# A decoder layer on one core: the first normalisation reads a transposed copy of x instead of transposing it on TensorE

## The chip, the cores and the metric

The kernel runs on one core of one Trainium2 chip. A core has TensorE (PE in the profile, with its weight loads as PEld), VectorE (DVE), ScalarE (ACT), GpSimd (POOL) and SyncE (SP, which here only issues transfers), and 16 DMA engines that they all share. The metric is the device time of one execution in microseconds (us); lower is better. The time of a kernel is the median of its runs.

## The reference

One decoder layer over 256 tokens of 2048 channels, in float32. Only its first steps matter here:

```python
h = rmsnorm(x, norm_mix_pre[l])
proj = h @ w_in[l]
xr, yr, q, k, v, g_rnn, g_attn = jnp.split(proj, IN_OFFSETS, axis=-1)
...
q = rope(q.reshape(B, S, N_Q_HEADS, HEAD_DIM), positions)
k = rope(k.reshape(B, S, N_KV_HEADS, HEAD_DIM), positions)
...
def rmsnorm(x, g):
    xf = x.astype(jnp.float32)
    y = xf * lax.rsqrt(jnp.mean(xf * xf, axis=-1, keepdims=True) + RMS_EPS)
    return (y * g.astype(jnp.float32)).astype(x.dtype)
```

After that come a gated linear recurrence over xr and yr, sliding-window attention over q, k and v, the merge of both by the gates, an output projection and an MLP with 8192 hidden channels, each with its own normalisation.

## The kernel before

**Products in parts.** Every large product is made from float32 operands that are split in a high part (rounded to the type that TensorE multiplies in one pass) and a low part (the rest), and sums three of the four products of parts. For the weights the class `Stream` does this: it cuts each weight chunk of 128 partitions x 2048 numbers (1 MiB) into two halves of 512 KiB, loads them in a fixed order on SP's queue (`load_to`, L76), and splits each into `whi` (a copy on ACT, L94 or L103) and `wlo` (a subtraction on DVE, L95 or L111). Halves 0 to 9 have rooms of their own; from half 10 on there is a ring of four (`WRAW`). The split halves have rings of six (`WHALF`). `ahead(j)` splits up to half j + 5 and asks for loads up to ten halves past j, as the rings allow.

**The activations.** TensorE contracts over the partitions, so x has to stand with its channels on the partitions, as 16 tiles of 128 channels x 256 tokens: `hT`, again in a high and a low part, already multiplied by the gain g of the normalisation (`gcol`). The factor 1/rms of each token is not in hT; it is put in behind the products.

**The beginning, before.** x comes in as it lies, tokens on the partitions (`x_nat`, two blocks tb of 128 tokens, in four quarters of 512 channels each), interleaved on SP's queue with the first weight halves. `turn(tb, q)` transposes one quarter of a block on TensorE (four transposes of 128x128, L375) into PSUM. `part(tb, q)` makes the parts of hT from PSUM: high on ACT (L382), low on DVE (L385), one instruction for each tile of 128 channels and block of 128 tokens, 32 on each engine. `kv_step(j)` takes the weight half j and two channel tiles, and makes 12 products of 128x128 by 128x512 (L396): eight with `whi` and then four with `wlo`. Eight such steps make keys and values. The transposes for the steps 2q + 2 and 2q + 3 stand between the steps 2q and 2q + 1. Most of this is held in program order by `keep_in_program_order` (`pin`): such an instruction stays behind the one written before it on its engine. What is not pinned is ordered when the program is built, by when it is expected to be ready.

**The squares.** The sums of squares of x for 1/rms are taken from x_nat ahead of the last kv step: block 0 in four instructions on ACT (L405), block 1 in four on DVE (L403).

**The pass behind it.** `b_pass512` runs 8 weight halves of 12 products each (L294, L296, L298), first for a group of gates (`g`), then for a group of queries (`q`). After each half of a gate pass it calls `pump`, which runs the next piece of the generators that wait: the first is `keys_values`, which calls `first_norm` (sum and root of the squares with `rms`, L357 to L359; 1/rms into the rotary tables cc and ss, L445; the spread of 1/rms over all partitions by a product with ones, L448, and its copy to `rT`), and for each token block copies the values (L519), rotates the keys (`rope`, L505 to L509) and transposes them on TensorE (`pk`, L526) into `kT`. The small inputs (positions, frequencies, sinks, per-channel vectors) are loaded on SP's queue behind the first 14 weight halves.

Of the kernel before, what the change touches and what calls it, by code (L numbers as in the profile page):

```python
# [30 lines left out]
NH, NKV, HD = 32, 4, 64  # L31
# [132 lines left out]
EXTRA = 5  # L164


def layer(tc, x, g_pre, pos_t, pos_row, inv_freq, vecs, sinks, gains, w_kv, w_q, w_xy, w_rg, w_g, w_rp, w_ap, w_out,
          w_up, w_dn, out):
    nc = tc.nc
    ctx = ExitStack()  # L170
# [7 lines left out]
    mm = nc.tensor.matmul  # L178
# [43 lines left out]
    def bank(pool, name):  # L222
        return pool.tile([P, 512], F32, tag=pool.name, name=name)
# [100 lines left out]
    def t2(name, dt=F32):  # L324
        return pa.tile([P, 512], dt, tag="t2", bufs=T2, name=name)

    x_nat = [flat(unit(f"x{tb}", F32)) for tb in range(TB)]
# [4 lines left out]
    gcol = const.tile([P, KT], F32, name="gcol")  # L332
    nc.scalar.dma_start(gcol, g_pre)

    for q in range(4):
        nc.sync.dma_start(x_nat[0][:, quarter(q)], x_v[0][:, quarter(q)])
        if q == 0:
            ws.load_to(1)
        last = nc.sync.dma_start(x_nat[1][:, quarter(q)], x_v[1][:, quarter(q)])
        with tc.issue_after(last.ins):  # L340
            ws.load_to(2 * q + 2)
# [8 lines left out]
    nc.vector.memset(ones, 1.0)  # L350
# [15 lines left out]
        mm(warm[:, 0:P], ones, ones, start=True, stop=True)  # L366
    hT = units("hT")
    pin = ws.pin = tc.keep_in_program_order
    ps_t = {}

    def turn(tb, q):
        ps = ps_t[tb, q] = bank(psm, "ptr")
        for i in range(4):
            k = 4 * q + i
            pin(nc.tensor.transpose(ps[:, i * P : i * P + P], x_nat[tb][:, k * P : k * P + P], ident))  # L375

    def part(tb, q, ks=range(4)):
        t = slice(tb * P, tb * P + P)
        ps = ps_t[tb, q]
        for i in ks:  # L380
            g = gcol[:, 4 * q + i : 4 * q + i + 1]
            pin(nc.scalar.activation(hT[q][:, i, 0, t], ps[:, i * P : i * P + P], AF.Copy, scale=g))  # L382
        for i in ks:
            g = gcol[:, 4 * q + i : 4 * q + i + 1]
            pin(nc.vector.scalar_tensor_tensor(hT[q][:, i, 1, t], ps[:, i * P : i * P + P], g,  # L385
                                               hT[q][:, i, 0, t].bitcast(F32), ALU.mult, ALU.subtract))

    kv = [bank(psb, f"kv{tb}") for tb in range(TB)]

# [8 lines left out]

    def squares(tb):
        for q in range(4):  # L400
            x, into = x_nat[tb][:, quarter(q)], sq[:, 0, tb, q : q + 1]
            if tb:
                pin(nc.vector.scalar_tensor_tensor(t2("j"), x, 1.0, x, ALU.mult, ALU.mult, accum_out=into))  # L403
            else:
                pin(nc.scalar.activation(t2("j"), x, AF.Square, accum_out=into))  # L405

    turn(0, 0)
    turn(1, 0)
    part(0, 0, (0, 1))
    ws.split_high()  # L410
    part(1, 0, (0, 1))
    ws.split_low()
    for tb in range(TB):
        part(tb, 0, (2, 3))
    ws.split_to(2)
    for q in range(4):
        kv_step(2 * q)
        if q < 3:
            turn(0, q + 1)
            turn(1, q + 1)  # L420
            part(0, q + 1)
            part(1, q + 1)
            ws.split_to(2 * q + 4)
        else:
            ws.pin = lambda i: i
            squares(0)
            squares(1)
            ws.split_to(2 * q + 4)
        kv_step(2 * q + 1)
    ws.ahead(ws.at - 1)  # L430
    r0, r0h = [], []
    rT = pa.tile([P, S], F32, name="rT")

    def first_norm():

        pr = bank(psm, "pr")
        spread = t2("spread")
        for tb in range(TB):
            r = rms(tb, 0)
            half = st[:, 16 + tb : 17 + tb]  # L440
            nc.vector.tensor_scalar(half, r, 0.5, None, ALU.mult)
            r0.append(r)
            r0h.append(half)
            for t in (cc, ss):
                nc.vector.tensor_scalar(t[:, tb], t[:, tb], r, None, ALU.mult)  # L445
            dg = spread[:, tb * P : tb * P + P]
            nc.vector.tensor_scalar(dg, ident, r, None, ALU.mult)
            mm(pr[:, tb * P : tb * P + P], ones, dg, start=True, stop=True)  # L448
        nc.scalar.copy(rT, pr[:, 0:S])

    pos_i = pa.tile([P, TB], I32, name="pos_i")
    nc.sync.dma_start(pos_i, pos_t)
    ifr = pa.tile([P, 32], F32, name="ifr")
    nc.sync.dma_start(ifr, inv_freq.partition_broadcast(P))
    sink = pa.tile([P, NH], F32, name="sink")
    nc.sync.dma_start(sink, sinks.partition_broadcast(P))
    vec = pa.tile([P, 8, KT], F32, name="vec")
    nc.sync.dma_start(vec, vecs.rearrange("p (a b) -> p a b", a=8))


    mask1 = pa.tile([P, S], F32, name="mask1")
    nc.gpsimd.memset(mask1, 0.0)
# [51 lines left out]

    def keys_values(banks):
        yield
        first_norm()
        for tb in range(TB):
            nc.scalar.activation(v_sb[:, tb, :], banks[tb][:, 256:512], AF.Copy, scale=r0[tb])  # L519
            k2 = t2("k2")  # L520
            k4 = k2.rearrange("p (g c d) -> p g c d", g=NKV, c=2)
            rope(banks[tb][:, 0:256], tb, NKV, [k4[:, :, 0, :], k4[:, :, 1, :]])
            yield
            ps = bank(psm, "pk")
            for g in range(NKV):
                nc.tensor.transpose(ps[:, g * P : g * P + P], k2[:, g * P : g * P + P], ident)  # L526
# [711 lines left out]
def lay_out(inp):  # L1238


    def a_type(w):
        k, n = w.shape
        return np.ascontiguousarray(w.reshape(KT, P, n // P, P).transpose(2, 1, 0, 3)).reshape(n // P, P, 2048)

    def b_type(w, cols):
        k, n = w.shape
        per = 2048 // cols
        t = w.reshape(k // (per * P), per, P, n // cols, cols).transpose(3, 0, 2, 1, 4)
        return np.ascontiguousarray(t).reshape(-1, P, 2048)
# [23 lines left out]
    return {  # L1273
        "x": np.asarray(inp["x"]).reshape(S, D),
        "g_pre": per_channel(g("norm_mix_pre")),
        "pos_t": pos.T,
        "pos_row": pos.reshape(S),
        "inv_freq": (10000.0 ** (-np.arange(0, HD, 2, dtype=np.float64) / HD)).astype(np.float32),
        "vecs": np.concatenate(vecs, axis=1),
        "sinks": g("attn_sinks").reshape(NKV, 4, 2).transpose(0, 2, 1).reshape(NH),  # L1280
        "gains": np.stack([g(n) for n in ("norm_mix_pre", "norm_mix_post", "norm_mlp_pre", "norm_mlp_post")]),
        "w_kv": b_type(kv, 512),
        "w_q": b_type(q, 512),
        "w_xy": a_type(np.concatenate([xr, yr], axis=1)),
        "w_rg": np.ascontiguousarray(rg).reshape(4, P, 2048),
        "w_g": b_type(gg, 512),
        "w_rp": b_type(g("w_rnn_proj"), 512),
        "w_ap": b_type(g("w_attn_proj"), 512),
        "w_out": b_type(g("w_out"), 1024),
        "w_up": a_type(g("w_mlp_up")),  # L1290
        "w_dn": np.concatenate([down(w_dn[:4096]), down(w_dn[4096:])]),
    }
# [15 lines left out]
```

## Time and profile before

| what | value |
|---|---|
| runs | 1514.89, 1511.7, 1516.5 us; median 1514.89 us |
| span of the profiled execution | 1515.7 us |
| TensorE clock granted | 0.998 |
| PE busy | 1493.5 us (99%), 7600 instructions |
| DVE busy | 1102.2 us (73%) |
| ACT busy | 829.2 us (55%) |
| HBM read | 288.60 MB, 195 GB/s over the span |

The profile is that of one execution. A row of the timeline gives the start, the time from the first to the last instruction merged in the row, the engine, the line, the operation, out<-in, the shapes and the count, and in brackets the idle time just ahead of it with what ended it. A matmul's row shows its whole way through the array, so its time is longer than the distance to the next one; the pace of TensorE is read from the starts. Groups of instructions show the busy time and the mean of one in ns, and behind it the idle time of the engine ahead of them.

### The profile page before, as it was taken

To read this page: it belongs to the slowest core of one execution; us is meant where nothing else is said; L and a number is where in the kernel's file an instruction comes from. 1 tells how busy PE (TensorE), PEld (TensorE's weight loads), DVE (VectorE), ACT (ScalarE), POOL (GpSimd) and SP (SyncE) were. 2 spreads that over 40 slices of the span, in tenths; PEclk is the share of its full clock that TensorE was granted. 3 is DMA by queue.
4 is the path that set the end of the run, shared out by engine and by line. 5 is a ranking of instruction groups with operands and counts; after the bars stand their busy time and mean duration, and the time that the engine had idled before them with its cause. 6 is when DMAs were issued, how large, how long until landed. Compare 5 with 4: busy or idle time off the path is not lost.

```text
span 1515.7 us, 20016 instructions
## 1 busy us (share of the span) xinstructions
PE 1493.5 (99%) x7600; PEld 1259.8 (83%) x7600; DVE 1102.2 (73%) x1377; ACT 829.2 (55%) x1143; POOL 5.5 (0%) x11
## 2 busy tenths in 40 slices
PE   9999999999999999999999999999999999999996
PEld 7787778788888888888888888888888888888875
DVE  6666677858769966555667866798886666688897
ACT  6554654646566766443355655555454455555543
POOL 0000000000000000000000000000000000000001
PEclk9999999999999999999999999999999999999999
DMA  6645445465646565655764756566657555566564
GB/s 253 218 144 187 142 131 170 153 196 166 217 159 215 174 209 196 191 183 194 268 225 137 271 183 193 185 203 213 219 195 239 194 188 188 193 236 213 195 209 174
DMA packets 82895, 296.19 MB, mean 195 GB/s; under 512 B 9712, under 2 KB 9968, under 8 KB 81648
## 3 DMA queue, kind: packets, MB, share of 16 engines
q1 hardware_dynamic: 79056, 284.43, 57.4%
q10 hardware_dynamic: 3744, 10.50, 1.9%
q8 instruction: 59, 0.97, 0.2%
q14 instruction: 36, 0.29, 0.1%
HBM read 288.60 MB, written 6.29 MB: 195 GB/s over the span
## 4 chain that ended last, share of the span: by engine, by line
PE 82%; DVE 9%; DMA 4%; ACT 2%; issue 2%; DVEq 0%; SPq 0%; ACTq 0%
PE ps L256 21%; PE ps L254 11%; PE dQ L1084 4%; DMA wraw<-in_w_dn 4%; PE pp L294 4%; PE pp L296 4%; PE pp L298 4%; PE g L294 3%; DVE wlo L95 3%; PE g L298 3%; PE g L296 3%; PE s L1084 3%; PE dP L1084 2%; PE q L296 2%; PE q L298 2%; PE q L294 2%
## 5 line engine op out<-in xcount | busy, mean ns | idle before, releaser
L94 ACT CAST whi<-wraw 128x1024 fp32r<-128x1024 f32 x523 | 544.6, 1053 | 567.5 <-PE ps L256 123.7
L95 DVE TENSOR_TENSOR wlo<-wraw,whi 128x1024 fp32r<-128x1024 f32 x523 | 632.8, 1221 | 301.9 <-ACT whi L94 295.2
L256 PE MATMUL ps<-h2T,whi 128*128 128x512 f32 x960 | 223.9, 390 | 0.0
L256 PEld LDWEIGHTS ps<-h2T,whi 128*128 128x128 f32 x960 | 178.2, 188 | 35.6
L256 PE MATMUL ps<-hT,whi 128*128 128x512 f32 x512 | 121.3, 391 | 0.0
L254 PEld LDWEIGHTS ps<-h2T,wlo 128*128 128x128 f32 x960 | 119.1, 192 | 2.3
L254 PE MATMUL ps<-h2T,wlo 128*128 128x256 f32 x960 | 119.9, 283 | 0.0
L256 PEld LDWEIGHTS ps<-hT,whi 128*128 128x128 f32 x512 | 94.7, 188 | 20.1 <-issue 1.5
L1084 PE MATMUL dQ<-whi,uT 128*128 128x512 f32 x288 | 106.9, 389 | 0.0
L294 PE MATMUL g<-whi,hT 128*128 128x512 f32 x256 | 101.2, 395 | 0.0
L296 PE MATMUL g<-wlo,hT 128*128 128x512 f32 x256 | 100.0, 391 | 0.1
L298 PE MATMUL g<-whi,hT 128*128 128x512 f32 x256 | 99.8, 390 | 0.0
L254 PE MATMUL ps<-hT,wlo 128*128 128x256 f32 x512 | 64.9, 283 | 0.0
L254 PEld LDWEIGHTS ps<-hT,wlo 128*128 128x128 f32 x512 | 63.8, 191 | 1.2
L1084 PEld LDWEIGHTS dQ<-whi,uT 128*128 128x128 f32 x288 | 54.1, 188 | 11.2
L1084 PE MATMUL dQ<-wlo,uT 128*128 128x512 f32 x144 | 56.4, 391 | 1.2 <-DVE wlo L95 1.1
L294 PEld LDWEIGHTS g<-whi,hT 128*128 128x128 f32 x256 | 48.1, 188 | 10.6 <-issue 1.0
L298 PEld LDWEIGHTS g<-whi,hT 128*128 128x128 f32 x256 | 48.1, 188 | 10.2
L296 PEld LDWEIGHTS g<-wlo,hT 128*128 128x128 f32 x256 | 48.1, 188 | 9.9 <-DVE wlo L95 0.5
L1084 PE MATMUL dCs<-whi,uT 128*128 128x512 f32 x144 | 54.1, 389 | 0.0
L1084 PE MATMUL dP<-whi,uT 128*128 128x512 f32 x144 | 54.1, 389 | 0.0
L130 DVE TENSOR_TENSOR tlo<-t,thi 128x1536 fp32r<-128x1536 f32 x28 | 49.2, 1756 | 5.5 <-ACT thi L129 5.3
(280 smaller groups left out, 2462.1 us busy)
## 6 DMA issues: line engine op xcount, KB each, us to landing
wraw<-in_w_up SPq DMA_DIRECT2D x128, 512.0 KB, 4.1
wraw<-in_w_dn SPq DMA_DIRECT2D x128, 512.0 KB, 4.8
wraw<-in_w_g SPq DMA_DIRECT2D x64, 512.0 KB, 4.7
wraw<-in_w_xy SPq DMA_DIRECT2D x64, 512.0 KB, 4.5
wraw<-in_w_q SPq DMA_DIRECT2D x32, 512.0 KB, 4.4
wraw<-in_w_ap SPq DMA_DIRECT2D x32, 512.0 KB, 4.6
wraw<-in_w_rp SPq DMA_DIRECT2D x32, 512.0 KB, 4.1
wraw<-in_w_out SPq DMA_DIRECT2D x32, 512.0 KB, 4.9
```

The source lines that it names most:

```text
L94: self.pin(self.nc.scalar.copy(hi, src))
L95: self.pin(self.nc.vector.tensor_tensor(lo, src, hi.bitcast(F32), ALU.subtract))
L130: v.tensor_tensor(lo, t, hi.bitcast(F32), ALU.subtract)
L254: mm(ps[:, f, 1, :], w, a[:, 0, :], start=False, stop=j == 1 and k == 7)
L256: mm(ps[:, f].rearrange("p a b -> p (a b)"), w, a.rearrange("p a b -> p (a b)"), start=kt == 0, stop=j == 3 and k == 7)
L294: mm(banks[tb][n], a[:, 0, t], hi[:, n * 512 : n * 512 + 512], start=first, stop=False)
L296: mm(banks[tb][n], a[:, 0, t], lo[:, n * 512 : n * 512 + 512], start=False, stop=False)
L298: mm(banks[tb][n], a[:, 1, t], hi[:, n * 512 : n * 512 + 512], start=False, stop=last)
L1084: mm(b, a[x], w[y], start=not begun and i == 0, stop=tail and i == 2)
```

## The change

The host hands in x a second time, transposed and cut in four loads: `x_t[q]` is 128 partitions (channels) x 4 channel tiles x 256 tokens. The kernel loads that first (`xts`, the tiles `xt(k)`), between the weight halves, the first quarter in two loads. `part(k)` now makes the parts of one channel tile for all 256 tokens, from SBUF: 16 instructions on ACT and 16 on DVE instead of 32 and 32. The transposes (`turn`) are gone. x as it lies is still loaded, in eight tiles of 128x512 of the pool `t2`, behind twelve weight halves and the small inputs. The squares are taken from these in place, inside the second piece of `keys_values`, so in the gate pass, pinned; in the third and fourth piece stand the values and the rotation of the keys, in the fifth and sixth the transposes of the keys, and in the seventh the product that spreads 1/rms. An ACT instruction on a constant is put in ahead of everything (the first `activation` loads ACT's table).

```diff
+    def load_xt(a, b):
+        q, c = a // 4, slice(a % 4 * S, a % 4 * S + (b - a) * S)
+        nc.sync.dma_start(xt(a, b - a), x_t[q][:, c])
+
+    ws.load_to(1)
+    load_xt(0, 2)
+    load_xt(2, 4)
+    ws.load_to(2)
+    for q in range(1, 4):
+        load_xt(4 * q, 4 * q + 4)
+        ws.load_to(2 * q + 2)
+    ws.load_to(12)
...
+    x_nat = [[t2("xq") for q in range(4)] for tb in range(TB)]
+    for tb in range(TB):
+        for q in range(4):
+            nc.sync.dma_start(x_nat[tb][q], x_v[tb][:, quarter(q)])
     ws.load_to(2 * EXTRA + WRAW)
...
+    nc.scalar.activation(st[:, 30:31], eps, AF.Copy)
...
+    def part(k):
+        q, i, g, src = k // 4, k % 4, gcol[:, k : k + 1], xt(k)
+        pin(nc.scalar.activation(hT[q][:, i, 0, :], src, AF.Copy, scale=g))
+        pin(nc.vector.scalar_tensor_tensor(hT[q][:, i, 1, :], src, g, hT[q][:, i, 0, :].bitcast(F32), ALU.mult,
+                                           ALU.subtract))
...
+    for j in range(8):
+        if j == 0:
+            ws.split_high()
+        for i in range(2):
+            part(2 * j + i)
+        if j:
+            ws.split_high()
+        ws.split_low()
+        kv_step(j)
     ws.ahead(ws.at - 1)
...
-            dg = spread[:, tb * P : tb * P + P]
-            nc.vector.tensor_scalar(dg, ident, r, None, ALU.mult)
-            mm(pr[:, tb * P : tb * P + P], ones, dg, start=True, stop=True)
-        nc.scalar.copy(rT, pr[:, 0:S])
+            nc.vector.tensor_scalar(spread[:, tb * P : tb * P + P], ident, r, None, ALU.mult)
+        return spread
+
+    def spread_r0(spread):
+        pr = bank(psm, "pr")
+        for tb in range(TB):
+            t = slice(tb * P, tb * P + P)
+            mm(pr[:, t], ones, spread[:, t], start=True, stop=True)
+        nc.scalar.copy(rT, pr[:, 0:S])
...
     def keys_values(banks):
         yield
-        first_norm()
+        squares(0)
+        squares(1)
+        ws.pin = lambda i: i
+        spread = first_norm()
+        yield
+        turned = []
         for tb in range(TB):
             nc.scalar.activation(v_sb[:, tb, :], banks[tb][:, 256:512], AF.Copy, scale=r0[tb])
             k2 = t2("k2")
             k4 = k2.rearrange("p (g c d) -> p g c d", g=NKV, c=2)
             rope(banks[tb][:, 0:256], tb, NKV, [k4[:, :, 0, :], k4[:, :, 1, :]])
+            turned.append(k2)
             yield
+        for tb, k2 in enumerate(turned):
             ps = bank(psm, "pk")
             for g in range(NKV):
                 nc.tensor.transpose(ps[:, g * P : g * P + P], k2[:, g * P : g * P + P], ident)
             nc.scalar.copy(kT[:, :, tb * P : tb * P + P], ps.rearrange("p (g t) -> p g t", g=NKV))
             yield
+        spread_r0(spread)
```

More of the change, by code (lines that the diff above doesn't have):

```diff
@@ L164, with layer @@
 EXTRA = 5
-def layer(tc, x, g_pre, pos_t, pos_row, inv_freq, vecs, sinks, gains, w_kv, w_q, w_xy, w_rg, w_g, w_rp, w_ap, w_out,
+def layer(tc, x, x_t, g_pre, pos_t, pos_row, inv_freq, vecs, sinks, gains, w_kv, w_q, w_xy, w_rg, w_g, w_rp, w_ap, w_out,
           w_up, w_dn, out):
@@ L325, in t2, with xt @@
         return pa.tile([P, 512], dt, tag="t2", bufs=T2, name=name)
-    x_nat = [flat(unit(f"x{tb}", F32)) for tb in range(TB)]
+    xts = [flat(unit(f"xt{i}", F32)) for i in range(2)]
+    def xt(k, n=1):
+        return xts[k // 8][:, k % 8 * S : (k % 8 + n) * S]
     x_v = x.rearrange("(t p) d -> t p d", p=P)
@@ L333, in layer @@
     nc.scalar.dma_start(gcol, g_pre)
[L335 to L341, printed above, removed]
+    def load_xt(a, b):
[9 more added lines that the diff above has]
+    ws.load_to(12)
+    pos_i = pa.tile([P, TB], I32, name="pos_i")
+    nc.sync.dma_start(pos_i, pos_t)
+    ifr = pa.tile([P, 32], F32, name="ifr")
+    nc.sync.dma_start(ifr, inv_freq.partition_broadcast(P))
+    sink = pa.tile([P, NH], F32, name="sink")
+    nc.sync.dma_start(sink, sinks.partition_broadcast(P))
+    vec = pa.tile([P, 8, KT], F32, name="vec")
+    nc.sync.dma_start(vec, vecs.rearrange("p (a b) -> p a b", a=8))
+    x_nat = [[t2("xq") for q in range(4)] for tb in range(TB)]
+    for tb in range(TB):
+        for q in range(4):
+            nc.sync.dma_start(x_nat[tb][q], x_v[tb][:, quarter(q)])
     ws.load_to(2 * EXTRA + WRAW)
@@ L368, in layer @@
     pin = ws.pin = tc.keep_in_program_order
[L369 to L386, printed above, removed]
+    def part(k):
[3 more added lines that the diff above has]
+                                           ALU.subtract))
     kv = [bank(psb, f"kv{tb}") for tb in range(TB)]
@@ L400, in squares @@
         for q in range(4):
-            x, into = x_nat[tb][:, quarter(q)], sq[:, 0, tb, q : q + 1]
+            x, into = x_nat[tb][q], sq[:, 0, tb, q : q + 1]
             if tb:
-                pin(nc.vector.scalar_tensor_tensor(t2("j"), x, 1.0, x, ALU.mult, ALU.mult, accum_out=into))
+                pin(nc.vector.scalar_tensor_tensor(x, x, 1.0, x, ALU.mult, ALU.mult, accum_out=into))
             else:
[L405 to L429, printed above, removed]
+                pin(nc.scalar.activation(x, x, AF.Square, accum_out=into))
+    for j in range(8):
[7 more added lines that the diff above has]
+        kv_step(j)
     ws.ahead(ws.at - 1)
@@ L1274, in lay_out @@
         "x": np.asarray(inp["x"]).reshape(S, D),
+        "x_t": np.ascontiguousarray(np.asarray(inp["x"]).reshape(S, 4, 4, P).transpose(1, 3, 2, 0)).reshape(4, P, 4 * S),
         "g_pre": per_channel(g("norm_mix_pre")),
```

9 lines of the change are left out of this document (removed).

## The prediction, made before the changed kernel was run

> **What bounds the kernel now.** First the page's totals, then the timeline of the first 60 us for TensorE, then the same for the engines that feed it.
>
> ```profile
> span 1515.7 us, 20016 instructions
> PE 1493.5 (99%) x7600; PEld 1259.8 (83%) x7600; DVE 1102.2 (73%) x1377; ACT 829.2 (55%) x1143; POOL 5.5 (0%) x11
> ```
>
> TensorE is busy for 99% of the span, so only two things can shorten it: fewer instructions on PE, or PE gaps closed. The change touches only what lies ahead of 60 us. Behind that PE stays busy, and the weight loads follow its pace (195 GB/s on average against 406 in the row of loads below), so what is won at the beginning is carried to the end. The beginning on PE:
>
> ```profile
> 1.08 4.63 PE L366 MATMUL warm<-ones 128*128 128x128 f32 x20 [1.08 <-DVE ones L350]
> 7.96 0.66 PE L375 MATMUL ptr<-ident,x 128*128 128x128 f32 x4 [1.42 <-DMA x<-in_x]
> 8.37 2.38 PE L396 MATMUL kv<-whi,hT 128*128 128x512 f32 x8
> ...
> 18.81 1.03 PE L375 MATMUL ptr<-ident,x 128*128 128x128 f32 x8
> 19.60 2.07 PE L396 MATMUL kv<-whi,hT 128*128 128x512 f32 x8
> ...
> 32.13 1.98 PE L396 MATMUL kv<-whi,hT 128*128 128x512 f32 x8
> 33.95 1.07 PE L396 MATMUL kv<-wlo,hT 128*128 128x512 f32 x4
> 34.85 0.39 PE L294 MATMUL g<-whi,hT 128*128 128x512 f32 x1
> ```
>
> From the starts: eight products take 33.95 - 32.13 = 1.82 us and four 34.85 - 33.95 = 0.90, so one product 0.227 and a step of twelve 2.72. The eight steps are worth 21.8 us, yet lie between 8.37 and 34.85, that is 26.5 us. Three groups of eight transposes stand between them, each 19.60 - 18.81 = 0.79 us, together 2.4. The other 2.3 us are waits, which the waits of this stage name for PE's weight loads:
>
> ```profile
> PEld kv L396 <- ACT whi L94: 1.3, 3, 0.4
> PEld kv L396 <- DVE wlo L111: 0.8, 1, 0.8
> PEld kv L396 <- ACT hT L382: 0.4, 1, 0.4
> ```
>
> The next gaps are at the start of the gate pass and at the product that spreads 1/rms:
>
> ```profile
> 35.34 0.50 PE L296 MATMUL g<-wlo,hT 128*128 128x512 f32 x1
> 43.86 0.39 PE L298 MATMUL g<-whi,hT 128*128 128x512 f32 x1
> 45.10 0.49 PE L448 MATMUL pr<-spread,ones 128*128 128x128 f32 x2 [0.85 <-DVE spread L447]
> 54.57 0.66 PE L526 MATMUL pk<-ident,k 128*128 128x128 f32 x4
> ```
>
> The second gate product starts 0.49 us behind the first instead of 0.227: 0.26 lost to the half `wlo`, late because the squares on DVE stood ahead of it. The spread was waited for 0.85.
>
> **The change part by part.** *Start of the first step.* The loads as issued, then the time to landing of the first four of SP's queue (KB, us), then the rate from 12 us on:
>
> ```profile
> 0.74 0.38 SPq L336 DMA_DIRECT2D x<-in_x  x1
> 1.17 0.42 SPq L76 DMA_DIRECT2D wraw<-in_w_kv  x1
> 1.64 0.42 SPq L339 DMA_DIRECT2D x<-in_x  x1
> 2.11 0.43 SPq L76 DMA_DIRECT2D wraw<-in_w_kv  x1
> x<-in_x SPq DMA_DIRECT2D x1, 256.0 KB, 3.8
> wraw<-in_w_kv SPq DMA_DIRECT2D x1, 512.0 KB, 4.7
> x<-in_x SPq DMA_DIRECT2D x1, 256.0 KB, 6.3
> wraw<-in_w_kv SPq DMA_DIRECT2D x1, 512.0 KB, 7.1
> 12.00:25.00 13.00, 12.96 (x64) 10.23 (x63) 10.03 (x22) 8.11 (x20) 0.00 (x0) 1.00 1.03 406
> ```
>
> So 256 KB had landed at 4.5 us, 768 at 5.9, 1024 at 7.9, 1536 at 9.2; from there 512 KB take 1.29 us at 406 GB/s. The changed queue has weight half 0 (512 KB) first, then channel tiles 0 and 1 (to 768), tiles 2 and 3 (to 1024), half 1 (to 1536). Half 0 lands between 4.5 and 5.9, and I take the middle, 5.2; the tiles 5.9, 7.9; half 1 9.2; the next quarter of x 10.5, half 2 11.8, half 3 13.1. What ACT and DVE need:
>
> ```profile
> L382 ACT ACTIVATE hT<-ptr,gcol 128x128 fp32r<-128x128 f32 x32 | 8.9, 379 | 7.7 <-PE ptr L375 7.6 <-DVE hT L385 0.2
> L94 ACT CAST whi<-wraw 128x1024 fp32r<-128x1024 f32 x21 | 21.4, 1074 | 6.4 <-DVE turns L480 3.3 <-PE g L298 2.5 <-ACT rT L449 0.4
> L95 DVE TENSOR_TENSOR wlo<-wraw,whi 128x1024 fp32r<-128x1024 f32 x20 | 23.8, 1218 | 1.8 <-ACT whi L94 1.8
> L405 ACT ACTIVATE j<-x 128x512 f32<-128x512 f32 x4 | 2.5, 676 | 0.0
> L403 DVE SCALAR_TENSOR_TENSOR j<-x 128x512 f32<-128x512 f32 x4 | 2.5, 684 | 0.0
> L519 ACT ACTIVATE v_sb<-kv,st 128x256 f32<-128x256 f32 x2 | 0.8, 466 | 0.0
> L505 DVE TENSOR_TENSOR ra<-kv,cc 128x256 f32<-128x256 f32 x2 | 0.8, 415 | 0.0
> ```
>
> The new 128x256 parts appear nowhere before. On ACT they lie between 379 ns (128x128) and 676 (128x512); I take 466, the row of that very size. On DVE the upper end is 684 and I take 415, again that size. ACT then splits half 0 from 5.2 to 6.25, makes tile 0 by 6.7, and PE starts there: 1.7 us before 8.37 (1.0 if half 0 lands at 5.9). ACT's first table load, which waited for the gain before, now lies in ACT's idle time ahead of half 0.
>
> *The eight steps.* Per step ACT needs 2 x 0.47 + 1.07 = 2.0 us and DVE 2 x 0.42 + 1.22 = 2.1; at the upper ends 2.4 and 2.6. All are below PE's 2.72. The loads, 768 KB a step, need 1.94. So PE sets the pace, except at first: step 0 waits 0.2 for its low half (DVE: two parts to 7.5, then 1.22), ends at 9.6; half 1 is split at 9.2 + 1.05 = 10.25, a wait of 0.65; step 1 ends at 13.0, when half 2 is split (12.85). Six more steps end at 29.3, against 34.85: 5.5 us, namely 1.7 from the start, 2.4 from the transposes, 1.4 from waits (2.3 less 0.85).
>
> Weighed against the Trainium skill ("TensorE: Matmul & The Clock Gate", Part 4, PE-mode transpose): it gives some 275 ns for one transpose in a kernel. By it the 24 transposes would be worth 6.6 us and the whole sum some 4 us more. The starts above give 0.10 each, because they follow each other in the pipeline; a duration is not a price here.
>
> *Squares and loads moved.* The squares leave the front of the gate pass, so its second product no longer waits: 0.26. x as it lies is 2 MiB more to load, 5.2 us of the queue. It goes behind twelve halves, landing at 26.0, so it lands at about 31.2, and weight halves 12, 13 and 14 at 32.5, 33.8 and 35.1. PE wants half 12 at 29.3 + 4 x 2.72 = 40.2 and its split takes 2.3, so 5 us of cover remain; without it, each us later would be a us of PE. SP's small loads go ahead of x and nobody waits for SP.
>
> *The spread and the turned keys.* The product with ones is kept, at the end of the first pieces; its wait of 0.85 goes. What is late next is the chain to the turned keys: squares (pinned on ACT and DVE behind the split of half 14), root, tables, rotation. PE's four `pk` transposes stand in order among the gate products, and whatever is behind them in PE's queue waits too: all gate products. How long, nobody can read from before. Lower end: 0. The nearest rows: the spread was placed too early by 0.85, the keys' weight load by 0.3:
>
> ```profile
> PEld pk L526 <- DVE k L509: 0.3, 1, 0.3
> ```
>
> I take 0.7, between the two, and put the upper end in the rivals. Sum: 5.5 + 0.26 + 0.85 - 0.7 = 5.9 us. From the profiled span of 1515.7 that gives 1509.8; the median of the runs lies 0.8 lower, so **1509.0**.
>
> **The rivals.** *The turned keys stay at their written place* (20%). There `pk` stands behind five halves, 60 products: 29.3 + 13.6 = 42.9. The chain: half 14 split on DVE by 37.4; four squares on DVE 2.5, to 39.9. Then these rows:
>
> ```profile
> 41.24 0.21 DVE L357 TENSOR_REDUCE st<-sqs 128x1 f32<-128x4 f32 x2
> 42.70 1.28 ACT L358 ACT_TABLE_LOAD   x1
> 54.23 0.28 DVE L509 TENSOR_TENSOR k<-ra,rb 128x128 f32<-128x128 f32 x1
> ```
>
> Unhindered, I estimate sums, table and roots at 2.2, tables and spread 0.8, rotation 1.5, and one or two splits of 1.22 between: ready at 45.6 to 46.9, so a wait of 2.7 to 4.0. With 3.3 the gain is 6.6 - 3.3 = 3.3: 1511.6. For it: both waits of this kind before were too early, never too late. Against: `pk` was written behind 36 products and stood behind (54.57 - 34.85)/0.227, some 80, so the order follows readiness.
>
> *Slower: the chain is as long as before* (9%). From the sum at 41.24 to the rotated keys at 54.5 it took 13.3 us, with splits, angles and a second table load between its steps. From 39.9 that is 53.2, and up to 1.5 more if the small loads thin the queue; with `pk` at 42.9 PE waits 10.3 to 11.8. At 11.5 the kernel loses 4.9: 1519.8. It is slower at all from a wait of 6.6. Against: the angles can be done while DVE waits for halves 12 to 14, and the splits that stood between the steps now run ahead.
>
> *The loads don't come in the written order* (8%), so that the change doesn't do what it says. If the 2 MiB of later weights or the 2 MiB of x, or both, pass the last quarter of transposed x, that is 5.2 to 10.4 us later. It lands at 18.3 and is wanted at 22, so PE waits 1.5 to 6.7, and the time is 1510.5 to 1515.7, say 1513. Before, a queue order was forced by hand there, which is gone; against it, nothing holds the earlier loads back.
>
> *The clock falls back* (5%). The transposes at 5.5 kept PE occupied behind the warm-up, which ends at 5.7; now it idles 1.0 us, or 1.7 at the late landing. Warm-up matmuls start every 0.23 us for 128 columns, a quarter of the kv products' 512 at the same distance. If the first step ran at half pace it would cost 2.7: gain 3.2, 1511.7. Against: PE idled for 1.42 ahead of the transposes at 7.96, and the clock, the column behind the busy times, was 1.00 there:
>
> ```profile
> 5.00:10.00 5.00, 3.58 (x18) 2.64 (x17) 1.29 (x5) 3.75 (x9) 0.00 (x0) 1.00 0.99 302
> ```
>
> The Trainium skill ("TensorE: Matmul & The Clock Gate", Part 1) lets the clock fall after an idle window of about 3.4 us; by that rule, which the 1.42 agrees with, this happens only if the first tile comes past 9.
>
> **How the numbers follow.** The forecast has 58%. Its own range is 1507.0 to 1510.7: the wait from 0 to 1.3, the start 0.7 later, and a us for the median of three runs that spread over 4.8. A measurement of this kernel tells about 0.3%, 4.5 us, from no change, so faster means under 1510.3. Faster: nearly all of the forecast and a quarter of the load rival, 58%. Same: the written place, the clock, most of the load rival, the forecast's edge: 32%. Slower by over 0.3%: the long chain and a rest, 10%. The range goes from 1506.8 to 1514.3; it leaves out the long chain and the worst of the loads.
>
> **What would show it.** The first kv product at 6.7 to 7.4; the first gate product near 29.3, with no transposes and only two waits ahead of it, both before 10.3; 128x256 parts near 0.47 and 0.42 us; no wait at the spread; `pk` waiting under 1.3 us; half 14 landed by 36.6; the clock at 1.00. The prediction is wrong if `pk` waits over 2 us, if kv steps wait for tiles of x past the second, or if the first 60 us go as forecast and the time is given back behind them.

## The result, and the profile after

| | before | after |
|---|---|---|
| median of the runs | 1515.07 us (4 runs, 1511.7 to 1516.5) | 1519.6 us (4 runs, 1518.92 to 1521.69) |
| ratio, with 95% interval | | 1.0035 [1.0023, 1.0047] |
| span of the profiled execution | 1515.7 us | 1517.7 us |
| first product of the first gates | 34.85 us | 29.27 us |
| first product of the first queries | 59.65 us | 63.90 us |
| first product of the third gates | 135.2 us | 140.7 us |

By the medians the kernel is 4.5 us slower, and the interval of the ratio lies above 1; 5.9 us of gain were forecast. All differences of medians in this study are under half a per cent. The last three rows, read from the timelines of TensorE, tell where: the gate pass starts 5.6 us earlier and ends 4.2 us later, and 1.3 us more are lost before the third gates. From there to the products at 302 us before and 307 us after the distance stays at 5.4 to 5.5. The two spans differ by only 2.0, since the rest of the kernel behind these products, which is the same code, took 3.5 us less in the one profiled execution than in the other; over all the profiles of this study it lies between 1210 and 1215 us, so shifts at a fixed place tell more here than spans.

The totals of the page of after:

```profile
span 1517.7 us, 19931 instructions
PE 1488.2 (98%) x7568; PEld 1258.9 (83%) x7568; DVE 1100.5 (73%) x1361; ACT 827.9 (55%) x1128; POOL 5.5 (0%) x11
PEclk9899999999999999999999999999999999999999
```

PE is busy 5.3 us less, the 32 transposes among it, in a span that is longer; and the second slice of the clock (38 to 76 us) has an 8 where the rest has 9. The timeline of TensorE in after (start, time, engine, operation, count, idle time before it):

```profile
7.14 2.28 PE L406 MATMUL kv<-whi,hT 128*128 128x512 f32 x8 [1.43 <-ACT hT L394]
...
29.27 0.39 PE L294 MATMUL g<-whi,hT 128*128 128x512 f32 x1
...
43.61 0.50 PE L296 MATMUL g<-wlo,hT 128*128 128x512 f32 x1 [0.35 <-DVE wlo L95]
...
44.41 0.40 PE L296 MATMUL g<-wlo,hT 128*128 128x512 f32 x1
53.84 1.09 PE L523 MATMUL pk<-ident,k 128*128 128x128 f32 x4 [9.03 <-DVE k L499]
...
55.15 0.63 PE L294 MATMUL g<-whi,hT 128*128 128x512 f32 x1
55.58 0.63 PE L296 MATMUL g<-wlo,hT 128*128 128x512 f32 x1
...
60.72 0.61 PE L448 MATMUL pr<-spread,ones 128*128 128x128 f32 x4
...
63.90 0.39 PE L294 MATMUL q<-whi,hT 128*128 128x512 f32 x1
```

Up to 43 us all goes as forecast: eight steps without a transpose, the gate pass at 29.27, its 65 products ahead of `pk` at 0.227 us. Then PE stands still for 9.03 us, since the rotated keys, which `pk` transposes, are not there and the remaining products stand behind `pk` in its queue. Behind the pause two products lie 55.58 - 55.15 = 0.43 us apart instead of 0.227. The stages of after (length, busy time of PE, PEld, DVE, ACT, POOL, granted clock, DMA share, GB/s) show both the clock and a thin stretch of loads:

```profile
28.00:30.00 2.00, 2.00 (x11) 1.65 (x10) 0.80 (x1) 0.00 (x0) 0.00 (x0) 1.00 0.75 153
30.00:32.00 2.00, 2.00 (x11) 1.65 (x10) 0.00 (x0) 0.00 (x0) 0.00 (x0) 1.00 0.78 243
32.00:34.00 2.00, 2.00 (x10) 1.68 (x9) 0.00 (x0) 0.00 (x0) 0.00 (x0) 1.00 1.00 396
48.00:50.00 2.00, 0.00 (x0) 0.00 (x0) 1.93 (x13) 1.81 (x5) 0.00 (x0) 0.50 0.41 131
54.00:56.00 2.00, 2.00 (x7) 1.72 (x7) 2.00 (x6) 0.58 (x1) 0.00 (x0) 0.50 0.65 209
```

From 30 to 34 us DVE and ACT do nothing at all: they wait for half 12. Then, in the timelines of ACT and DVE in after, the chain to the keys:

```profile
35.60 1.05 ACT L94 CAST whi<-wraw 128x1024 fp32r<-128x1024 f32 x1 [8.06 <-DMA wraw<-in_w_g]
36.67 1.28 ACT L476 ACT_TABLE_LOAD   x1
40.95 0.26 ACT L476 ACTIVATE turns<-ang 128x64 f32<-128x64 f32 x1 [3.00 <-DVE ang L474]
41.26 1.99 ACT L94 CAST whi<-wraw 128x1024 fp32r<-128x1024 f32 x2
...
37.83 0.16 DVE L465 CAST posf<-pos_i 128x2 f32<-128x2 int32 x1
...
47.05 0.15 DVE L379 TENSOR_REDUCE st<-sqs 128x1 f32<-128x4 f32 x1
...
53.41 0.28 DVE L499 TENSOR_TENSOR k<-ra,rb 128x128 f32<-128x128 f32 x1
```

Half 12 came at 35.6. Behind its split stands the sine's table load on ACT; the sine then waits 3.00 us for the angles, which DVE begins only behind the low part of half 12, at 37.83. The splits of halves 13 and 14 stand behind the sine (41.26), the squares behind these splits, and the rotation behind the squares: keys at 53.7. PE had reached the place of `pk` in its queue at 44.8.

**The account of the gate pass.** It took 59.65 - 34.85 = 24.8 us before and 34.6 after. The 9.8 more are 9.03 for `pk`, 0.35 at half 13, whose split is late by the same chain, and some 1.5 at half clock (six gate products at 0.43, which cost 1.2 us more, and the transposes), less the waits of 0.26 and 0.85 that are gone.

### The profile page after: what moved, and what is told of

Its sections match the earlier page's. It is cut to its first block, busy times and chain, and to the rows that moved or that the text cites. A ratio compares the mean times of both kernels' runs of the same rounds, so it can differ in the third digit from the quotient of the medians.

```text
span 1517.7 us, 19931 instructions
## 1 busy us (share of the span) xinstructions
PE 1488.2 (98%) x7568; PEld 1258.9 (83%) x7568; DVE 1100.5 (73%) x1361; ACT 827.9 (55%) x1128; POOL 5.5 (0%) x11
## 4 chain that ended last, share of the span: by engine, by line
PE 79%; DVE 10%; DMA 6%; ACT 3%; issue 2%; SPq 0%; DVEq 0%; ACTq 0%
PE ps L256 21%; PE ps L254 11%; PE dQ L1082 4%; PE pp L296 4%; PE pp L294 4%; PE pp L298 4%; DMA wraw<-in_w_dn 4%; DVE wlo L95 3%; PE g L298 3%; PE g L294 3%; PE g L296 3%; PE s L1082 3%; PE dP L1082 2%; PE q L296 2%; PE q L298 2%
## 5 line engine op out<-in xcount | busy, mean ns | idle before, releaser
L95 DVE TENSOR_TENSOR wlo<-wraw,whi 128x1024 fp32r<-128x1024 f32 x516 | 624.7, 1220 | 318.3 <-ACT whi L94 314.0
L94 ACT CAST whi<-wraw 128x1024 fp32r<-128x1024 f32 x516 | 538.2, 1051 | 572.8 <-PE ps L256 133.5
L298 PEld LDWEIGHTS g<-whi,hT 128*128 128x128 f32 x256 | 48.5, 190 | 10.2
L296 PEld LDWEIGHTS g<-wlo,hT 128*128 128x128 f32 x256 | 48.4, 189 | 10.3 <-DVE wlo L95 0.8
```

What stands on the lines that cost most here:

```text
L94: self.pin(self.nc.scalar.copy(hi, src))
L95: self.pin(self.nc.vector.tensor_tensor(lo, src, hi.bitcast(F32), ALU.subtract))
L296: mm(banks[tb][n], a[:, 0, t], lo[:, n * 512 : n * 512 + 512], start=False, stop=False)
L298: mm(banks[tb][n], a[:, 1, t], hi[:, n * 512 : n * 512 + 512], start=False, stop=last)
```

## The experiments

All are timed in several rounds against the kernel before on the same chips, whose medians were 1515.23 and 1515.34 us beside them. "Squares summed" is the start of DVE's first sum of the squares (`TENSOR_REDUCE`), in us; where x comes behind the halves (after, e1 to e4, e6) the squares end just there, in the others they end 5 to 7 us earlier and the sum waits behind other work of DVE. "Shift" is the start of the first product at 301.8 us of before's profile (a group behind everything that differs) in the experiment, less 301.8; after has +5.5. Shift and median belong to different executions.

| run | squares summed | `pk` behind | its wait | shift | median, us | ratio to before [95%] |
|---|---|---|---|---|---|---|
| after | 47.05 | 65 products | 9.03 | +5.5 | 1519.60 | 1.0035 [1.0023, 1.0047] |
| e1 | 47.2 | 120 | 0 | -2.9 | 1513.94 | 0.9986 [0.9975, 0.9997] |
| e2 | 40.85 | 65 | 1.96 | -0.5 | 1515.19 | 0.9996 [0.9985, 1.0008] |
| e3 | 41.98 | 65 | 3.59 | +1.6 | 1516.39 | 1.0002 [0.9989, 1.0014] |
| e4 | 46.4 | 60 | filled | +5.1 | 1520.49 | 1.0037 [1.0026, 1.0048] |
| e5 | 36.9 | 60 | 0.99 | -3.2 | 1513.43 | 0.9987 [0.9978, 0.9996] |
| e6 | 46.9 | 65 | 9.03 | +6.0 | 1522.69 | 1.0048 [1.0035, 1.0062] |
| e7 | 37.1 | 60 | 2.63 | -1.4 | 1515.27 | 0.9996 [0.9986, 1.0007] |
| e8 | 40.7 | 78 | 0.98 | -0.6 | 1514.56 | 0.9994 [0.9985, 1.0003] |
| e9 | 37.6 | 84 | 0 | -6.0 | 1510.17 | 0.9964 [0.9951, 0.9978] |
| e11 | 36.7 | 84 | 0 | -6.8 | 1509.58 | 0.9962 [0.995, 0.9975] |

**e1: the turning of the keys later.** Four empty pieces ahead of the transposes of the keys, so that `pk` is asked for later in PE's order; nothing else.

```diff
+        for _ in range(4):
+            yield
         for tb, k2 in enumerate(turned):
```

> Edit: the changed kernel, with four empty pieces more ahead of the two that transpose the rotated keys, so that TensorE meets these transposes only behind 120 products of the passes instead of 65. Theory A (the loss is the place of the transposes in TensorE's queue against a chain that ends at 53.6 us): no wait of pk, no fall of the clock; instead the first query products wait some 2.7 us, since the two banks of keys and values that they need come free at 54.4 us (end of the rotation's reading) while the gate pass ends at 51.4. The 63.9 us at which the queries start now, less 1.3 for the transposes and the spread that move behind that point, less 54.1, make 8.5 us of gain on the changed kernel: 1511 us median. Rival B (the loss lies in the 2 MiB of additional loads or behind 64 us): the wait of pk goes, but the time stays within 2 us of the changed kernel's 1519.6.

The wait is gone, and from 140 us on the kernel is 8.4 us ahead of after (-2.9 against +5.5), although the chain is as late as in after. So the 9 us are a matter of where `pk` stands against that chain, and the 2 MiB of additional loads, which are the same in e1, do not by themselves make after slower. By the medians e1 gains 5.7 us on after, where 8.5 were forecast. The place is no free choice: the first queries, at 52.97, are held up at their next bank, which the rotation still reads. From the timeline of TensorE in e1:

```profile
7.52 2.88 PE L406 MATMUL kv<-whi,hT 128*128 128x512 f32 x8 [1.81 <-ACT hT L394]
...
54.67 0.47 PE L294 MATMUL q<-whi,hT 128*128 128x512 f32 x1 [0.87 <-DVE rb L496]
```

The first row shows something else: the first eight products take 2.88 instead of 2.28 us. The clock was at half from 9.0 to 12.4, and the gate pass began at 31.2 instead of 29.3.

**e2: angles and small loads earlier.** The other cure: an earlier chain with `pk` where it is. The small loads go ahead of four weight halves, and angles and sines ahead of the splits of halves 8 to 14.

```diff
     ws.load_to(2 * q + 2)
-    ws.load_to(12)
...
     nc.sync.dma_start(vec, vecs.rearrange("p (a b) -> p a b", a=8))
+    ws.load_to(12)
...
         kv_step(j)
+    posf = small("posf", [P, TB])
+    pin(nc.vector.tensor_copy(posf, pos_i))
...
+        nc.vector.tensor_scalar(ss[:, :, i, :], sn, 1.0 - 2.0 * i, None, ALU.mult)
     ws.ahead(ws.at - 1)
```

> Edit: the changed kernel, with the small loads (positions, frequencies, sinks, vectors) moved ahead of weight halves 8 to 11 and the angle work on VectorE and ScalarE (13 small instructions, two sines and their table load) moved ahead of the splits of halves 8 to 12. Theory A1 (a good part of the chain's lateness is the angle work, which starts only behind the split of half 12 and holds the splits of halves 13 and 14 back on ScalarE from 36.7 to 41.3): the squares end some 4.4 us earlier, pk waits 4.6 instead of 9.0, half a us to a us less at the low clock: 1514 to 1515 us. Rival A2 (only the load of x counts, the angles hide behind it): the squares end within 1 us of where they do now and pk waits over 8 us: 1519 us.

The timeline of ACT in e2, then that of TensorE:

```profile
32.69 1.05 ACT L94 CAST whi<-wraw 128x1024 fp32r<-128x1024 f32 x1 [2.49 <-DMA wraw<-in_w_g]
...
36.18 1.05 ACT L94 CAST whi<-wraw 128x1024 fp32r<-128x1024 f32 x1 [1.17 <-DMA wraw<-in_w_g]
```

```profile
47.81 0.63 PE L523 MATMUL pk<-ident,k 128*128 128x128 f32 x4 [1.96 <-DVE k L499]
```

The squares end 6.2 us earlier (40.85), and the wait falls by 7.1, of which 1.0 only because PE came to `pk` later, after a start at half clock (gate pass at 31.0). Half 12 is there at 32.7 instead of 35.6, where the forecast had it, with the same bytes ahead of it: the four small loads, 97 KB, had cost 2.9 us of the queue where they stood. In after they lay in one row in front of x. The issues on SP's queue in after, and of the transfers the KB and the time to landing:

```profile
16.59 0.33 SPq L352 DMA_DIRECT2D pos_i<-in_pos_t  x1
...
20.43 0.33 SPq L358 DMA_DIRECT2D vec<-in_vecs  x1
21.71 7.07 SPq L362 DMA_DIRECT2D xq<-in_x  x8
28.83 2.90 SPq L76 DMA_DIRECT2D wraw<-in_w_g  x4
...
vec<-in_vecs SPq DMA_DIRECT2D x1, 64.0 KB, 6.7
...
pos_i<-in_pos_t SPq DMA_DIRECT2D x1, 1.0 KB, 10.0
```

SP issues one about every 1.28 us there, as transfers land, and a transfer of 1 KB takes up a place for 10 us like one of 512. When the halves ahead had landed, little was on its way, which is the stretch of 153 and 243 GB/s; x went out until 28.8 and half 12 only then. e2 moved two things, so it does not say how much of the 6.2 us is the queue's and how much the angles'; e3 does in part.

**e3: x behind half 13.** Angles and small loads as in after, x two halves later in the queue.

```diff
+    ws.load_to(2 * EXTRA + WRAW)
     x_nat = [[t2("xq") for q in range(4)] for tb in range(TB)]
     for tb in range(TB):
         for q in range(4):
             nc.sync.dma_start(x_nat[tb][q], x_v[tb][:, quarter(q)])
-    ws.load_to(2 * EXTRA + WRAW)
```

> Edit: the changed kernel, with the 2 MiB of x as it lies loaded behind weight halves 12 and 13 instead of ahead of them. Theory A2 (ScalarE and VectorE stand still from 28.5 to 36 us because half 12, which lands behind x, is next in their fixed order): half 12 is split by 29 us, the angles go into the time that was idle, and the squares wait for half 14 alone (35.6 us): they end near 40.4 instead of 47.1, pk waits 2.4 instead of 9.0 and the clock stays at 1.00: gain 6.6 + 1.5 = 8.1 us on the changed kernel, 1511.5 us. Rival A1 (the angle work is the larger part): the squares end later than 43 and pk waits over 5 us.

A miss in size. The timelines of ACT (splits of halves 12 and 14, and the sine) and of TensorE in e3:

```profile
27.90 1.05 ACT L94 CAST whi<-wraw 128x1024 fp32r<-128x1024 f32 x1 [0.52 <-PE kv L406]
...
33.24 0.26 ACT L476 ACTIVATE turns<-ang 128x64 f32<-128x64 f32 x1 [3.00 <-DVE ang L474]
...
37.30 1.05 ACT L94 CAST whi<-wraw 128x1024 fp32r<-128x1024 f32 x1 [2.71 <-DMA wraw<-in_w_g]
```

```profile
7.20 3.43 PE L406 MATMUL kv<-whi,hT 128*128 128x512 f32 x8 [1.48 <-ACT hT L394]
...
48.93 1.08 PE L523 MATMUL pk<-ident,k 128*128 128x128 f32 x4 [3.59 <-DVE k L499]
```

Half 12 is split at 27.9, and ACT waits the same 3.00 us for the angles; but half 13 is split by 34.6, and ACT then stands idle until half 14 comes at 37.3. The angles delay nothing here; in after they did, because half 12 was late. Half 14 came later than I had reckoned, the squares end at 41.98 and the wait is 3.59. It was enough for the clock to fall, for 6.8 us (47.6 to 54.4). The shift improves by 3.9 on after: 5.4 from the wait, less 1.2 at the start, where the first eight products took 3.43 us instead of 2.28 and the gate pass began at 30.4, and less part of the second spell. The clock's column shows 1.00 at that start, but the products start at half pace from the first on; no fall is on record there, and the clock's first record, at 10.1 us, is a rise. e4 starts in the same way (3.59 us; rise at 10.3).

**e4: the clock kept up.** 44 products of `ones` by `ones` that nobody reads, pinned ahead of `pk`, so that PE has work while it waits.

```diff
+        idle = bank(psm, "idle")
+        for i in range(44):
+            pin(mm(idle[:, 0:P], ones, ones, start=True, stop=True))
         for tb, k2 in enumerate(turned):
```

> Edit: the changed kernel, with 44 products of a constant with itself (128x128 float32, their result is read by nobody) on TensorE ahead of the first transposes of the keys, which fill 9.7 of the us in which TensorE waits. The transposes now stand behind 60 gate products instead of 65. Theory C (the wait of 9.0 us also costs clock: it fell to half from 47.0 to 57.2 us, and the products behind the wait start every 0.43 us instead of 0.23): the clock stays at 1.00, products behind pk at 0.23 from the first on; the queries start 1.5 us earlier, less 1.1 for the five products that now come behind: 63.5 against 63.9, and 1519 us. Rival (the clock's fall costs nothing because something else paces the products there): the pace behind pk stays at 0.43 and the queries start at 65.

The timeline of TensorE in e4:

```profile
44.10 9.98 PE L522 MATMUL idle<-ones 128*128 128x128 f32 x88
53.92 0.60 PE L526 MATMUL pk<-ident,k 128*128 128x128 f32 x4
54.28 0.48 PE L294 MATMUL g<-whi,hT 128*128 128x512 f32 x1
```

The clock stays at 1.00 and the products behind `pk` have their 0.40. Yet the queries start at 63.50, only 0.4 before after's: `pk` stands behind 60 products here, so five more lie behind the pause (1.1 us), and the idle products ran 0.9 us past the keys, which were there at 53.0. By the medians e4 is no faster than after. The clock behind the pause is the smaller part of the loss; the pause is the larger.

**e5: x before half 10, squares ahead of the gate pass.** As e2, and x as early as its rooms allow, so that the squares need wait for no half.

```diff
+    ws.load_to(10)
     x_nat = [[t2("xq") for q in range(4)] for tb in range(TB)]
...
+    ws.split_to(10)
+    squares(0)
+    squares(1)
+    ws.pin = lambda i: i
     ws.ahead(ws.at - 1)
...
         yield
-        squares(0)
-        squares(1)
-        ws.pin = lambda i: i
         spread = first_norm()
```

> Edit: the changed kernel, with the small loads and then the 2 MiB of x as it lies moved ahead (small loads behind weight half 7, x behind half 9), the angle work ahead of the splits of halves 8 and 9, and the squares directly behind these splits instead of in the second piece of the keys' work; everything else as in the changed kernel. Theory A (place and chain): squares end near 30 us, the root waits only for its place behind the split of half 14 on ScalarE, the first rotated keys are ready near 43.5, the transposes behind 60 products come at 43 to 44.5: pk waits 0 to 0.6 us, no fall of the clock in the gate pass, queries start at 52.5 plus what the start loses: 1511 us, or 1509 without the 1.2 us that all versions with the change lost near 113 us. Rival D (the 2 MiB of x cost their own time wherever they stand, since the weights behind them come late): the gate pass waits for halves 10 and 11, and the queries start past 55.

Short of the forecast: the squares end at 32.1 (30 expected), but DVE takes their sums only behind the low parts of four more halves, at 36.9, and the root follows at 39.6, behind the split of half 14. `pk` waits 0.99 (0 to 0.6 expected), and the queries start at 55.2. The median is 6.2 us below after's and 1.8 below before's. The gate pass begins at 30.8. Timelines of TensorE and of DVE, and the stages, in e5:

```profile
7.12 2.94 PE L406 MATMUL kv<-whi,hT 128*128 128x512 f32 x8 [1.62 <-ACT hT L394]
```

```profile
36.86 0.21 DVE L379 TENSOR_REDUCE st<-sqs 128x1 f32<-128x4 f32 x2
```

```profile
8.50:12.00 3.50, 3.50 (x10) 2.68 (x10) 3.37 (x7) 2.92 (x5) 0.00 (x0) 0.51 1.00 394
```

Again half clock at the start, behind a pause of 1.62 us: ten products in 3.5 us.

**e6: three more warm-up products.** After, with 13 pairs instead of 10 ahead of the first step, to close that pause.

```diff
-WARM = 10
+WARM = 13
```

> Edit: the changed kernel with 13 warm-up products instead of 10, so that TensorE is occupied to about 7 us instead of 5.7. Theory C2 (in the changed kernel the pause between the warm-up and the first step lets the clock rise late or fall again: in four experiments the clock was at half for 1 to 3.4 us between 6 and 12.4 us, and the gate pass began at 30.4 to 31.2 instead of 29.3): the clock rises once and stays, and the gate pass begins at 29.3 to 29.6. Rival (a matter of each execution, independent of the pause): the clock again rises past 9 us or falls between 7 and 12.5, and the gate pass begins past 30.3. Either way pk waits some 9 us as before: 1518 to 1520 us.

The timeline of TensorE in e6:

```profile
1.08 5.92 PE L388 MATMUL warm<-ones 128*128 128x128 f32 x26 [1.08 <-DVE ones L372]
7.26 2.28 PE L406 MATMUL kv<-whi,hT 128*128 128x512 f32 x8 [0.26 <-ACT hT L394]
```

The pause shrinks to 0.26 and the clock does not fall at the start, as in the profile of after, which had kept it without. The wait for `pk` is 9.03 again. The time came out 3 us over after's in four runs, above what was expected; the shift explains 0.5 of it, and the rest stays open.

**e7: e5 with e6's warm-up.**

> Edit: the two before together (x early, 13 warm-up products). Theory A and C2: queries start at 52 to 53, 1510 us, a gain on the kernel before of 5 us; rival: no better than x early alone.

A miss, and the most telling one. Timelines of TensorE and of ACT, and the stages, in e7:

```profile
45.83 0.65 PE L524 MATMUL pk<-ident,k 128*128 128x128 f32 x4 [2.63 <-DVE k L503]
```

```profile
37.31 1.05 ACT L94 CAST whi<-wraw 128x1024 fp32r<-128x1024 f32 x1 [1.37 <-DVE st L379]
38.38 1.28 ACT L380 ACT_TABLE_LOAD   x1
```

```profile
8.50:12.00 3.50, 3.50 (x17) 2.75 (x16) 3.50 (x6) 2.76 (x4) 0.00 (x0) 1.00 1.02 379
46.30:49.70 3.40, 3.40 (x11) 2.63 (x10) 3.12 (x7) 0.59 (x1) 0.00 (x0) 0.50 0.73 231
```

The start is right: 17 products where e5 had ten, the gate pass at 29.4 instead of 30.8. But the keys come when they came in e5 (45.7 against 45.4), since loads and splits set their time: the root's table load stands behind the split of half 14, which was asked for only at 33.6. (The row puts ACT's wait ahead of that split down to DVE's sums, which end at the same time.) PE reaches `pk` 1.4 us earlier and waits 1.6 longer, and 2.63 us of pause bring the clock down for 3.4 us: the queries begin at 57.0, against 55.2 in e5. An earlier start made the kernel later.

**e8: the pieces alone.** Before, with only the new division of `keys_values`: squares, transposes on TensorE and loads as before, but values and rotation first, then `pk`, then the spread.

```diff
-        first_norm()
+        spread = first_norm()
+        yield
+        turned = []
...
+            turned.append(k2)
             yield
+        for tb, k2 in enumerate(turned):
...
             yield
+        spread_r0(spread)
```

> Edit: the kernel before the change, with the new division of the keys' work alone: both rotations first, then the two transposes, then the product that spreads 1/rms; transposes of x, loads and squares as before. Theory A: the wait of 0.85 us at the spread goes and nothing else in the beginning: queries start at 58.7 instead of 59.7. Theory E (the 1.2 us that every version with the change lost near 113 us, waiting for softmax, comes from this division): the same loss appears here at the transposes of the probabilities of the first group; if it doesn't, it comes from the other parts.

The wait of 0.85 at the spread is gone, and `pk`, behind the same 78 products, now waits 0.98. The queries start 0.6 us earlier, but so does the gate pass (34.29 instead of 34.85), in this execution; the pass itself takes 24.75 us, as before. The division wins nothing and is harmless by itself, and so the harm comes from what it meets in after. The 1.4 us at 113 us (below) are not in e8.

**e9: e7 with `pk` two pieces later.** The two cures together.

```diff
+        for _ in range(2):
+            yield
         for tb, k2 in enumerate(turned):
```

> Edit: x early with 13 warm-up products, and two empty pieces more ahead of the transposes of the keys, so that they stand behind 84 and 96 products of the passes instead of 60 and 72. Theory A (with x early and the clock held the chain to the rotated keys ends at 45.7 us, set by the split of half 14; 84 products from 29.4 end at 48.5): no wait of pk, no fall of the clock, the query products find their banks free, queries start at 52.1 instead of 57.0; later only the 1.4 us at the transposes of the probabilities. Some 5.9 us less than the kernel before: 1509.3 us median. Rival B2 (what is won here is lost again behind 60 us): the offset against the kernel before at the second pass of queries (107.2 us there) shrinks below 4 us, or the median stays above 1512.

The timeline of TensorE in e9:

```profile
7.04 2.31 PE L406 MATMUL kv<-whi,hT 128*128 128x512 f32 x8 [0.98 <-ACT hT L394]
...
48.20 0.60 PE L526 MATMUL pk<-ident,k 128*128 128x128 f32 x4
...
101.70 1.23 PE L605 MATMUL pt<-ident,s 128*128 128x128 f32 x8 [1.43 <-DVE s L588]
```

No wait, no fall of the clock, the queries at 51.8. It beats both kernels: 1510.17, 5.2 us below before's median, and a shift of -6.0. That is about the 5.9 of the forecast, reached with x and the angles early, 13 warm-up pairs and `pk` behind 84 products. The last row is where the 1.2 to 1.3 us go that after loses at 113 us too: transposes of the probabilities (`pt`) stand behind 289 products there instead of 295, six products or 1.4 us too early.

**e11: the probabilities later too.** e9 with three empty pieces ahead of the first `pt` of three groups.

```diff
+        for _ in range(3 if g < 3 else 0):
+            yield
         turn_probs(0)
```

> Edit: the one before, and in the first three groups of heads three empty pieces more ahead of the transposes of the probabilities, which then stand behind 312 products instead of 289 (and likewise in the next two groups). Theory E2 (the 1.4 us near 113 us are the same kind of loss: the transposes stand six products earlier in TensorE's queue than in the kernel before, 289 against 295, and wait for a softmax that comes no sooner): these waits go in three groups, 1.4 us more in the first and as much in the other two, where the kernel before had them too: 1505 us. Rival (the softmax itself is late, the place doesn't matter): the wait moves along, and the time stays at that of the one before.

A miss. The waits of TensorE in e11, from 60 to 320 us, and the longest of the first kind in its timeline:

```profile
PE pt L605 <- ACT pT L607: 3.8, 3, 1.7
...
PE pt L605 <- DVE s L588: 1.5, 1, 1.5
```

```profile
120.80 0.66 PE L605 MATMUL pt<-ident,s 128*128 128x128 f32 x4 [1.74 <-ACT pT L607]
```

In e9 the second wait came four times, 5.8 us in all. Three of them are gone, and in their place `pt` waits for its own banks, which ACT's copies free; that the transposes, placed later, come too close together is the likely reason, not a tested one. The shift gains 0.8 on e9, and the medians can't be told apart.

## Why the prediction was wrong

*The start and the eight steps*: right, the exact 29.3 with some luck. The first product came at 7.14 (forecast 6.7 to 7.4), the first gate product at 29.27 (29.3), and the waits for `wlo` and for the spread are gone. Two small errors cancel: the start was 0.4 later than the 6.7 of the sum, and the eight steps lost 0.4 us where 0.85 of waits were reckoned. The Trainium skill ("TensorE: Matmul & The Clock Gate", Part 4) gives some 275 ns for a transpose; by it, as an estimate, the gate pass would have begun some 4 us earlier still. The measured 5.6 us agree with the distance of starts, 0.10 us each.

*"The squares end 39.9"*: wrong by 7.2, for two causes that the list of the moved loads and instructions should have shown. "SP's small loads go ahead of x and nobody waits for SP": nobody waits for SP, but half 12 waited 3.1 us for the places that the small loads held, 35.6 instead of 32.5. And the forecast costed the angles at nothing ("can be done while DVE waits for halves 12 to 14"): they are pinned behind half 12's low part, and ACT's sine stands ahead of the splits of halves 13 and 14. After the 3.1 us of half 12 that leaves some 4 us for them (an estimate, 7.2 less 3.1). e3 takes half 12's lateness away and e2 both; the squares end 5.1 and 6.2 us earlier.

*From the squares to the keys*: right. 45.6 to 46.9 less 39.9 was 5.7 to 7.0, and 47.05 to 53.7 are 6.6.

*"I take 0.7, between the two"*: this is the term of the sum that failed. The wait was 9.03 us, and some 1.5 us of low clock behind it, which the sum put at nothing. The reason given, "the order follows readiness", was read from one order that happened to be right. The order of PE is made when the program is built, by what is expected there: `pk` stood behind 65 products in after, in e2, in e3 and in e6, with keys ready at 53.7, 47.7, 48.8 and 53.5. Lateness of the chain was not a reason for the order to wait, and there was no reason for a wait to stay small. The forecast's own chain (45.6 to 46.9) would have given 0.8 to 2.1 us at that place (44.8); the rest, some 7 us, is the late squares, that is the small loads and the angles, both priced at nothing in the sum.

*The rivals.* The long chain, 1519.8 with a wait of 10.3 to 11.8, came nearest: the place is right, and PE did wait there for the keys. That its number fits (1519.6) is luck. It took the 13.3 us from the sum of the squares to the keys over from before, ready at 53.2; in after that stretch took 6.6, and the time was lost ahead of the sum, of which the rival had only the small loads, at up to 1.5. "The splits that stood between the steps now run ahead", held against it, was false: half 13 was split behind the sine. The clock fell too, behind `pk` rather than at the start in the profile of after, and at the start in e1, e2 and e5; e3 and e4 ran their first step at half pace without a fall on record. The 1.00 that the forecast read in the clock's column ahead of 10 us is therefore no proof at the start of a run: e3 and e4 show it too. The Trainium skill ("TensorE: Matmul & The Clock Gate", Part 1) lets it fall after an idle window of about 3.4 us; by that rule pauses of 1.62, 1.81 and 2.27 us at the start of e5, e1 and e2 should be harmless. They were not, so the condition that I took from it ("only if the first tile comes past 9") was wrong.

*"If the time is given back behind them"*: another 1.2 to 1.3 us were, at `pt`, a place that the forecast did not name.

## What to carry to other kernels

When an instruction that depends on a long chain stands in an in-order queue among work that does not, ask for the place where it was put and for the time of the chain, end to end, with every split, table load and pinned copy on the way; a small wait in an earlier order says nothing about the next. Price a load by the place it takes in the queue as well as by its bytes. And a gain ahead of a fixed late point is lost, or worse than lost if the longer pause costs the clock: move the consumer together with the producer.

## What the runs showed of the hardware

The clock fell behind pauses of PE shorter than the 9 us of after: 1.62, 1.81, 1.96, 2.27, 2.63 and 3.59 us (e5, e1, e2 twice, e7, e3). It did not fall behind pauses of 0.98, 1.30 and 1.43 (at the start of e9, e11 and after), nor behind 1.54 us (before, at 271 us), nor behind 1.74 us in e11. So the length of a pause alone does not decide between 1.6 and 1.8 us; what else does stays open. Once down, the clock stayed so for 3.4, 6.8 or 10.2 us (e1, e3, after), one, two or three times the same length. With ten warm-up pairs and no transposes five of six profiles ran the first step or two at half pace, and their eight steps took 1.1 to 1.6 us longer than in after; with 13 pairs none of four did, nor either of the two with the transposes. And a load of 1 KB on SP's queue took 10.0 us to land and held its place as long as one of 512 KB (9.1).
